# Last pair's attention, output weights and gate: an order of work written differently in a two-layer hybrid attention kernel

## The chip, the cores and the metric

One core of a Trainium2 chip runs the whole program: one launch, no other core takes part. The metric is the device time of an execution in microseconds (us), the median of several executions. Engines are named as in the profile: PE (TensorE's matmuls), PEld (its weight loads), DVE (VectorE), ACT (ScalarE), POOL (GpSimd), SP (SyncE, whose queue issues most of the loads).

## The reference

512 latent tokens and 256 context tokens of width 1024 go through two layers. Each layer modulates a root-mean-square norm with a shift and a scale, projects into three groups of attention heads and a gate path, and adds the gated output projection:

```python
mod = c_silu @ ada_w + ada_b
shift, scale, gate = jnp.split(mod, 3, axis=-1)
hx = rmsnorm(x, norm_w) * (1 + scale[:, None, :]) + shift[:, None, :]
px = split_cols(hx @ w_in)
...
ux = jnp.concatenate([ya, yb, yc_], axis=-1) * jax.nn.silu(px[9])
x = x + gate[:, None, :] * (ux @ w_out)
```

Group A is global attention (8 heads on 2 key heads, normalised and rotated), B is attention to a 2-D neighbourhood with a learned bias, C is a sliding window with a sink logit. All are softmax in float32. The context stream has its own modulation and is dropped after the first layer. The result is the final norm of the latent stream.

## The kernel before, in words

Everything is held transposed, features on the partitions and tokens along the free axis, and float32 products are made of three products of halves: each operand is split into a rounded high half and the rest (weights: `split`, line 239, `wh` by ACT at line 242 and `wl` by DVE or POOL at line 245).

**Stages of a layer.** A first stretch of projections; then the attention of twelve pairs of heads, each beside the projections for later pairs; then the output projection in eight blocks of 128 features. `PLAN` (line 33) lists for each step the pair whose attention runs, the projections beside it, and a couple of counts, for layer 0 and layer 1, of small pieces of modulation work. Its first entry has no pair (`None`), the second is pair (B, 0). `weave` (line 1371) interleaves the two generators in program order: it advances the attention while its cost so far, as a share of its planned cost `ta`, is not ahead of the other's share of `tb`. `with_ada` (line 1449) strews the counted pieces evenly over the projections' planned time.

**The order on the engines.** Instructions are written in program order, and a scheduler then orders each engine's queue by that order and by a model of when operands and buffers are ready. An extra edge, `after` (line 99), forces one instruction behind another of the same queue without a wait. In `weave`, `pace["at"]` is the name of an attention matmul that lies `CFG["lead"]` = 6.0 us of attention cost back; projections place every third of their products behind it (`paced`, line 291). The output products (`out_mm`, line 510) do not read it: only an explicit `behind_mm` counts.

**The last pair and the first output blocks.** The pair (C, 3) has no projections left beside it. The last line of `mixers` (1534) weaves its attention (with what is left of pair (A, 3)) with `head` (line 522): reloads of nine finished head-group results, and the products of output blocks 0 and 1 with eleven of the twelve feature groups, three products (cost 3 x 512/2400 = 0.64 us in the plan) for each group, 66 in all. The planned cost of the attention is 12.5 + 2.7 us in layer 0 and 12.5 us in layer 1, that of `head` 2 x 7.0 and 2 x 3.5. The twelfth group, which needs (C, 3) itself, is added when the block is finished.

**The output blocks of layer 0.** The loop over `d` in `body` (line 729) loads block `d`'s three weight tiles (`load_wo`, line 502: three loads of 256 KB on SP's queue into three staging buffers `ws`, then halves into five buffers `wh` and five `wl`, for blocks 5 to 7 into kept buffers), makes the latent tokens' block and for blocks 2 and 3 at once the context's (`block`, line 554). Blocks 0 and 1 come from `head`. From block 2 on it also works out layer 1's shift on DVE: `dot_begin` (line 692) loads two rows (`row`) and two pieces of modulation weights (`dw`, 512 KB each), `dot_step` makes two dot products (line 153) and loads the piece after next. These loads, and those of the class `Dots` (line 156), go through `aside` (line 141), which puts them behind the latest weight load written (`pace["sp"]`). Pieces, rows and kept weight halves share nine buffers. One step is made per block at block 2 and 3 for each stream, two at each block from the fifth on, until all eight are made.

**Layer 1's gate** is made by `Dots` in steps: sixteen dot products of half a row on DVE and two steps that only wait for the second half's row. Its rows and pieces take two of the four buffers `vt`, which the V tiles of the attention share. `PLAN` gives the first projections of layer 1 twelve steps and the stage of pair (B, 0) six.

Of the kernel before, what the change touches and what calls it, by code (L numbers as in the profile page):

```python
# [20 lines left out]
KT = 8  # L21
# [8 lines left out]
RPAD = 32  # L30
FT_ORDER = (4, 5, 6, 7, 0, 8, 1, 9, 2, 10, 3, 11)

PLAN = [(None, [("g", 0), ("b", 0), ("v", 0)], (0, 12)),
# [12 lines left out]
LATER = (5, 6, 7)  # L46
# [3 lines left out]
CFG = dict(lead=6.0, hp=600, hpf=600, pj=2, T=2, O=1, P=5, qt=5, kt=4, vt=4, gt=3, wh=5, ws=3, pt=3, bm=2, tA=1, OT=1, u=1, tl=1, ab="pj", tR=1, map={}, ada=2, h0=300, h1=1000, a0=9, H=2, hr=0, cp="A", cv="A", w0="D", w1="D", w2=(("D", "D"), ("D", "D")), hb="D", ws_="P")  # L50
# [13 lines left out]
def body(tc, xT, small, bcast, rpb, adaw, adat, wt, wf, wo, trigA, trigC, mskB, mskC, outT):  # L64
# [34 lines left out]
    def after(inst, name):  # L99

        tc.add_manual_dep(inst.ins, name, mybir.DependencyInfo(mybir.DependencyClass.NoSync,
                                                               mybir.DependencyReason.DATA), reason="bank")
# [133 lines left out]
    pace = {"at": None, "pe": None, "dve": None, "sp": None}  # L236
# [142 lines left out]
    with tc.tile_pool(name="p0", bufs=1, reuse_waits="tile") as p0:  # L379
        xs = {}  # L380
# [121 lines left out]
    def load_wo(l, d, room=None):  # L502
        w = {}
        for i in (1, 0, 2):
            st = wpool.tile([128, 512], F32, name="ws", bufs=CFG["ws"])
            pace["sp"] = nc.sync.dma_start(st, wo[l, d, i]).ins.name
            w[i] = split(st, (4, 128), room and room())
        return w

    def out_mm(p, w, ft, c0, n, behind_mm=None):  # L510
        wh, wl = w[ft // 4]
        r = ft % 4
        for i, (a, b) in enumerate(((wh, 0), (wh, 1), (wl, 0))):
            mm = nc.tensor.matmul(p[:, 0:n], a[:, r, :], ucols(ua[b][ft], c0, n),  # L514
                                  start=(ft == FT_ORDER[0] and i == 0), stop=(ft == FT_ORDER[-1] and i == 2))
            if i == 0 and behind_mm:
                after(mm, behind_mm)

    heads = {}
    out_banks = [pj, pj, lambda: Sbig[:, 0:512], psT, psT]  # L520
# [16 lines left out]
    for l in range(2):  # L537
        last = l == 1
        with tc.tile_pool(name=f"p1_{l}", bufs=1, reuse_waits="tile") as p1:
            mixers(tc, nc, l, last, p1, ps, const, dict(locals()))  # L540
        with tc.tile_pool(name=f"p2_{l}", bufs=1, reuse_waits="tile") as p2:
# [12 lines left out]
            def block(d, s, xs, sums, w):  # L554

                c0, c1 = SETS[s]
                n = c1 - c0
                xr = p2.tile([128, NT], F32, name="xr", bufs=3)
                nc.sync.dma_start(xr[:, 0:n], xsrc[l][d][:, c0:c1])
                if s == 0 and d in heads:  # L560
                    p, w = heads.pop(d)
                    fts = FT_ORDER[-1:]
                else:
                    p = out_bank()
                    fts = FT_ORDER
                for ft in fts:
                    out_mm(p, w, ft, c0, n)
                x = p2.tile([128, n], F32, name=f"xn{s}", bufs=8)
                res = nc.vector.scalar_tensor_tensor(x, p[:, 0:n], gate[:, d, s:s + 1], xr[:, 0:n],
                                                     op0=OP.mult, op1=OP.add)  # L570
                add_sq(sums, x, len(xs), n, p2)
                if s == 0:
                    xd = dram.tile([128, NT], F32, name=f"x1_{d}")
                    nc.scalar.dma_start(xd, x)
                    xsrc.setdefault(1, []).append(xd)
                xs[d] = x
                return res
# [108 lines left out]
            xs, sums = ({}, {}), ([], [])  # L686
# [25 lines left out]
            def dot_next():  # L712
                dot_step(dn["n"])
                dn["n"] += 1
# [11 lines left out]


            held = {}
            for d in range(KT):
                w = None  # L730
                if d not in heads:
                    w = load_wo(l, d, kept if d in LATER else None)
                if d == 2:
                    dot_begin()
                block(d, 0, xs[0], sums[0], w)
                for _ in range(0 if d < 2 else 2 if d > 3 else 1):
                    dot_next()
                if w is None or d in LATER or d not in AT_ONCE:
                    held[d] = w if d in LATER else None
                else:  # L740
                    block(d, 1, xs[1], sums[1], w)
                    dot_next()
            factors(0)
            n = 0
            for i, (d, w) in enumerate(sorted(held.items())):
# [11 lines left out]
def mixers(tc, nc, l, last, p1, ps, const, env):  # L757
    g_ = env
    en, pace = g_["en"], g_["pace"]
# [443 lines left out]
    class NearUnit(Unit):  # L1203
# [3 lines left out]

        PLAN = {1: (64, 0, 0, 256, {1: 0, 2: 128, 4: 256, 5: 384}),
# [3 lines left out]

        def scores(self):
            self.P = {}
            for i in (1, 2, 0, 3):
                k0, p0, loc, cx, _ = self.PLAN[i]
                nl = min(256, NT - k0, 128 * i + 192)
# [23 lines left out]
        def values(self):  # L1241
            O = psO()
            for n, kb in enumerate((4, 5, 1, 2, 3, 0)):
                qs = [i for i in range(4) if kb in self.PLAN[i][4]]
                T = psT()
# [89 lines left out]
    def chain(gens):  # L1335
        for g in gens:
            yield from g
# [30 lines left out]
                except StopIteration:  # L1368
                    lb = False

    def weave(a, ta, b, tb):

        xa = xb = 0.0
        la = a is not None
        past = []
        pace["pe"] = None
        while True:
            if la and xa * tb <= xb * ta:
                try:
                    xa += next(a)  # L1380
                    past.append((xa, pace["pe"]))
                except StopIteration:
                    la = False
            else:
                while len(past) > 1 and past[1][0] <= xa - CFG["lead"]:
                    past.pop(0)
                pace["at"] = past[0][1] if past and past[0][0] <= xa - CFG["lead"] else None
                try:
                    xb += next(b)
                except StopIteration as r:  # L1390
                    pace["at"] = None
                    if la:
                        for _ in a:
                            pass
                    return r.value
# [71 lines left out]
    TA = {"A": 16.5, "B": 12.5, "C": 12.5, None: 1.0}  # L1467
    TC = 0.0 if last else 2.7
# [7 lines left out]
    def any_bank():  # L1476
# [9 lines left out]
                g=b_g)  # L1486
# [7 lines left out]
    bmb = bias_b()  # L1494
    for pair, items, n_ada in PLAN:
        if pair is None and not last:

            items = items[1:] + items[:1]
        if pair is not None:
            kind, i = pair  # L1500
# [20 lines left out]
    def rest():  # L1521
        yield from attend(prev)
        yield from chain(pend)

    def urgent(gen):
        while True:
            with tc.high_priority(offset=CFG["hr"]):
                try:
                    x = next(gen)
                except StopIteration:  # L1530
                    return
            yield x

    weave(urgent(rest()), TA["C"] + TC, g_["head"](l, p1), CFG["H"] * (3.5 if last else 7.0))


def col_index():
# [95 lines left out]
```

## Time and profile before

| | us |
|---|---|
| median of 3 runs | 1215.67 |
| lowest, highest | 1214.95, 1218.88 |
| profiled execution, its own time | 1216.13 |
| its span, first to last instruction | 1214.3 |
| mean granted TensorE clock | 0.993 |

The profile is of one execution. Times within it count from the first instruction. A window row gives the length of a stretch, then each engine's busy time with the number of its instructions, the granted TensorE clock (1.00 is 2.4 GHz, 0.50 is 1.2 GHz), the busy share of the 16 DMA engines and what they moved in GB/s. A timeline row gives start and length, the engine and the source line, the operation with its output and inputs by the program's names, how many were merged, and in brackets the engine's idle time just before, with what ended it. Matmuls are pipelined: the start of one and the start of the next tell the pace, not the listed length.

### The profile page before, as it was taken

The page shows a single profiled execution, that of the slowest core. Times are in us where ns is not written, and L with a number is a line of the kernel's source. Part 1 is how long each engine was busy: PE and PEld are TensorE (multiplying, and loading weights), DVE is VectorE, ACT ScalarE, POOL GpSimd, SP SyncE. Part 2 cuts the span into 40 slices and gives each one's busy share as a digit, 9 for nine tenths or more (in the row PEclk, how much of TensorE's full clock was granted, in tenths as well). Part 3 has the DMA queues.
Part 4 walks back from the last instruction along what each step waited for, and adds up shares of the span by engine and source line. Part 5 has one row for each costly group of instructions (what it writes and reads, how often), then busy time and mean ns, then how long its engine had stood idle before and what let it go on. Part 6 is the DMA issues. An engine that isn't in the chain of part 4 may idle for free.

```text
span 1214.3 us, 21741 instructions
## 1 busy us (share of the span) xinstructions
PE 1160.1 (96%) x8016; PEld 1037.9 (85%) x8016; DVE 760.8 (63%) x1541; ACT 697.0 (57%) x1581; POOL 416.3 (34%) x511
## 2 busy tenths in 40 slices
PE   5999999999999999999889999999999999989997
PEld 3898999998898989988768999889989888878776
DVE  5667666765466665567577875666754665556553
ACT  5546555665566576587423544555666666667552
POOL 2432111233455454485100030211364554546001
PEclk9999999999999999999989999999999999999998
DMA  9552222312232112114085662333222112133052
GB/s 329 197 149 82 83 68 93 131 40 90 79 110 83 66 44 96 36 53 126 18 319 179 193 193 79 94 108 97 85 70 62 55 43 69 37 86 89 27 162 73
DMA packets 60826, 124.22 MB, mean 102 GB/s; under 512 B 7216, under 2 KB 13488, under 8 KB 60720
## 3 DMA queue, kind: packets, MB, share of 16 engines
q1 hardware_dynamic: 54768, 111.96, 29.0%
q10 hardware_dynamic: 5952, 10.88, 2.7%
q8 instruction: 63, 1.03, 0.4%
q14 instruction: 43, 0.35, 0.1%
HBM read 109.05 MB, written 11.14 MB: 99 GB/s over the span
## 4 chain that ended last, share of the span: by engine, by line
PE 82%; DVE 6%; ACT 4%; issue 3%; DMA 2%; POOL 1%; SPq 0%; ACTq 0%; DVEq 0%; POOLq 0%
PE pj L313 19%; PE pj L336 17%; PE Sbig L1034 9%; PE Obig L1034 9%; PE T L1039 8%; PE pj L514 5%; PE Sbig L514 3%; PE T L514 3%; PE T L336 2%; PE Sbig L425 1%; DVE ptl L1029 1%; ACT pth L783 1%; PE Sbig L336 1%; PE pj L425 1%; PE pj L209 1%
## 5 line engine op out<-in xcount | busy, mean ns | idle before, releaser
L1029 DVE TENSOR_TENSOR ptl<-T,pth 128x512 fp32r<-128x512 f32 (+2 forms) x312 | 180.8, 590 | 130.4 <-ACT pth L783 128.3
L783 ACT ACTIVATE pth<-T 128x512 fp32r<-128x512 f32 (+2 forms) x312 | 158.8, 519 | 138.7 <-PE T L1039 124.8
L336 PE MATMUL pj<-wh,hL 128*128 128x256 f32 x896 | 179.8, 287 | 0.1
L313 PE MATMUL pj<-hL,wh 128*128 128x512 f32 x544 | 175.9, 401 | 1.3 <-ACT wh L242 0.9
L1039 PE MATMUL T<-ident,P 128*128 128x128 f32 x1024 | 164.8, 273 | 4.8 <-DVE ptl L1029 2.6
L242 ACT ACTIVATE wh<-ws 128x512 fp32r<-128x512 f32 x192 | 119.3, 628 | 75.8 <-PE pj L313 14.4
L1034 PE MATMUL Sbig<-kt,qt 128*128 128x256 f32 (+1 forms) x864 | 157.6, 309 | 2.7 <-DVE negm L1177 1.8
L245 POOL TENSOR_TENSOR wl<-ws,wh 128x512 fp32r<-128x512 f32 x76 | 99.0, 1307 | 152.4 <-ACT wh L242 131.7
L336 PEld LDWEIGHTS pj<-wh,hL 128*128 128x128 f32 x896 | 144.3, 190 | 2.6 <-issue 0.6
L1034 PE MATMUL Obig<-pth,vt 128*128 128x256 f32 (+2 forms) x432 | 133.5, 319 | 8.0 <-ACT pth L783 7.1
L1039 PEld LDWEIGHTS T<-ident,P 128*128 128x128 f32 x1024 | 122.7, 140 | 17.3 <-DVE ptl L1029 3.9
L1034 PE MATMUL Obig<-ptl,vt 128*128 128x256 f32 (+2 forms) x432 | 131.8, 319 | 5.1 <-DVE ptl L1029 4.7
L1034 PEld LDWEIGHTS Sbig<-kt,qt 128*128 128x128 f32 x864 | 123.7, 189 | 13.3 <-DVE negm L1177 3.6
L336 PE MATMUL pj<-wl,hL 128*128 128x256 f32 x448 | 128.4, 287 | 0.0
L313 PEld LDWEIGHTS pj<-hL,wh 128*128 128x128 f32 x544 | 96.4, 189 | 17.6 <-ACT wh L242 1.3
L245 DVE TENSOR_TENSOR wl<-ws,wh 128x512 fp32r<-128x512 f32 x116 | 81.4, 709 | 46.5 <-ACT wh L242 41.0
L313 PE MATMUL pj<-hL,wl 128*128 128x512 f32 x272 | 107.2, 394 | 0.6 <-DVE wl L245 0.6
L1034 PEld LDWEIGHTS Obig<-pth,vt 128*128 128x128 f32 x432 | 81.6, 189 | 19.4 <-ACT pth L783 12.7
L1034 PEld LDWEIGHTS Obig<-ptl,vt 128*128 128x128 f32 x432 | 81.5, 189 | 16.3 <-DVE ptl L1029 11.3
L1409 POOL TENSOR_TENSOR bm<-wr,bm 128x192 f32<-128x192 f32 (+1 forms) x48 | 40.1, 864 | 142.9 <-DMA bm<-mskB_dram 130.2
L336 PEld LDWEIGHTS pj<-wl,hL 128*128 128x128 f32 x448 | 85.3, 190 | 0.4
L1129 DVE TENSOR_REDUCE negm<-Sbig 128x1 f32<-128x768 f32 x64 | 61.1, 955 | 33.9 <-ACT P L1131 20.3
(334 smaller groups left out, 2503.3 us busy)
## 6 DMA issues: line engine op xcount, KB each, us to landing
ws<-wf_dram SPq DMA_DIRECT2D x72, 256.0 KB, 2.9
ws<-wt_dram SPq DMA_DIRECT2D x72, 256.0 KB, 3.0
ada<-adaw_dram SPq DMA_DIRECT2D x32, 512.0 KB, 6.2
ws<-wo_dram SPq DMA_DIRECT2D x57, 256.0 KB, 2.7
bm<-mskB_dram SPq DMA_DIRECT2D x16, 576.0 KB, 3.8
dw<-adat_dram SPq DMA_DIRECT2D x8, 512.0 KB, 9.4
dots<-adat_dram SPq DMA_DIRECT2D x16, 256.0 KB, 3.7
u<-u ACTq DMA_DIRECT2D x9, 384.0 KB, 3.0
```

The source lines that it names most:

```text
L242: nc.scalar.activation(hi, src, AF.Copy)
L245: eng.tensor_sub(lo, src, hi.bitcast(F32))
L313: paced(nc.tensor.matmul(p[:, 0:n], a[:, r, :], cols(b[kt], c0, n), start=(i == 0), stop=(i == 23)), i)
L336: paced(nc.tensor.matmul(p[:, t * 256:(t + 1) * 256], tok(a[kt], t2 + t), b[:, r, :], start=(i == 0), stop=(i == 23)), i)
L425: mm = nc.tensor.matmul(out, a, b, start=begin, stop=(kt == KT - 1 and i == 2), skip_group_check=True)
L514: mm = nc.tensor.matmul(p[:, 0:n], a[:, r, :], ucols(ua[b][ft], c0, n), start=(ft == FT_ORDER[0] and i == 0), stop=(ft == FT_ORDER[-1] and ...
L783: nc.scalar.activation(out, src, AF.Copy)
L1029: i = nc.vector.tensor_sub(lo[:, 0:n], T[:, 0:n], hi[:, 0:n].bitcast(F32))
L1034: m = nc.tensor.matmul(*args, **kw)
L1039: m = nc.tensor.transpose(*args, **kw)
L1129: nc.vector.tensor_reduce(nm, S, axis=AX.X, op=OP.max, negate=True)
L1409: nc.gpsimd.tensor_add(b, src, b)
```

## The change

In layer 1 all eighteen steps of the gate go into the first projections, none beside (B, 0). The products of `head` read `pace["at"]`, and the last weave is given a lead of 3.0 us instead of 6.0 and the planned cost of `head` 2 x 8.0 us in layer 0 and 2 x 7.5 us in layer 1. In layer 0's output loop the weight load of block `d` + 1 is written at the start of step `d`, and the eight steps of dots follow a table: one behind each stream's block 2, one and two behind block 3, three behind block 4.

```diff
-PLAN = [(None, [("g", 0), ("b", 0), ("v", 0)], (0, 12)),
-        (("B", 0), [("b", 1)], (0, 6)),
+PLAN = [(None, [("g", 0), ("b", 0), ("v", 0)], (0, 18)),
+        (("B", 0), [("b", 1)], (0, 0)),
...
-            if i == 0 and behind_mm:
-                after(mm, behind_mm)
+            if i == 0 and (behind_mm or pace["at"]):
+                after(mm, behind_mm or pace["at"])
...
+            ws_ = {}
+
+            def load_next(d):
+
+                if d < KT and d not in heads:
+                    ws_[d] = load_wo(l, d, kept if d in LATER else None)
+
+            n_dots = {(2, 0): 1, (2, 1): 1, (3, 0): 1, (3, 1): 2, (4, 0): 3}
+
+            def out_block(d, s, w):
+                block(d, s, xs[s], sums[s], w)
+                for _ in range(n_dots.get((d, s), 0)):
+                    dot_next()
+
             for d in range(KT):
-                w = None
-                if d not in heads:
-                    w = load_wo(l, d, kept if d in LATER else None)
+                load_next(d + 1)
                 if d == 2:
                     dot_begin()
-                block(d, 0, xs[0], sums[0], w)
-                for _ in range(0 if d < 2 else 2 if d > 3 else 1):
-                    dot_next()
+                w = ws_.get(d)
+                out_block(d, 0, w)
                 if w is None or d in LATER or d not in AT_ONCE:
                     held[d] = w if d in LATER else None
                 else:
-                    block(d, 1, xs[1], sums[1], w)
-                    dot_next()
+                    out_block(d, 1, w)
...
-    def weave(a, ta, b, tb):
+    def weave(a, ta, b, tb, lead=CFG["lead"]):
...
-                while len(past) > 1 and past[1][0] <= xa - CFG["lead"]:
+                while len(past) > 1 and past[1][0] <= xa - lead:
                     past.pop(0)
-                pace["at"] = past[0][1] if past and past[0][0] <= xa - CFG["lead"] else None
+                pace["at"] = past[0][1] if past and past[0][0] <= xa - lead else None
...
-    weave(urgent(rest()), TA["C"] + TC, g_["head"](l, p1), CFG["H"] * (3.5 if last else 7.0))
+    weave(urgent(rest()), TA["C"] + TC, g_["head"](l, p1), CFG["H"] * (7.5 if last else 8.0), 3.0)
```

## Rows read from the trace of the kernel before

**Rows 1.** The page, part 1: busy time, share of the span, instructions

```profile
PE 1160.1 (96%) x8016; PEld 1037.9 (85%) x8016; DVE 760.8 (63%) x1541; ACT 697.0 (57%) x1581; POOL 416.3 (34%) x511
```

**Rows 2.** Windows, last pairs: length, busy PE PEld DVE ACT POOL, PEclk, DMA

```profile
565.00:605.00 40.00, 36.05 (x196) 29.36 (x196) 22.70 (x49) 20.75 (x51) 5.90 (x8) 0.96 0.09 29
...
1122.00:1160.00 38.00, 35.28 (x202) 29.03 (x201) 22.42 (x48) 19.77 (x44) 1.48 (x4) 1.00 0.08 28
...
590.00:595.00 5.00, 5.00 (x15) 3.92 (x16) 1.20 (x4) 0.76 (x2) 2.21 (x6) 0.66 0.00 0
```

**Rows 3.** The same view: stretches of earlier pairs, for comparison

```profile
500.00:540.00 40.00, 38.74 (x263) 34.60 (x262) 24.69 (x46) 31.24 (x75) 26.40 (x32) 1.00 0.17 48
...
1085.00:1095.00 10.00, 8.00 (x45) 6.20 (x45) 5.14 (x9) 7.93 (x19) 5.64 (x8) 1.00 0.31 81
```

**Rows 4.** Windows, output products of line 514 alone, before the last pair's scores

```profile
549.00:562.50 13.50, 8.28 (x32) 5.73 (x32) 1.00 0.68 187
...
1096.00:1121.50 25.50, 11.31 (x39) 6.95 (x39) 1.00 0.36 102
```

**Rows 5.** Timeline of PE, layer 0's output blocks

```profile
630.44 0.73 PE L514 MATMUL pj<-hL,wh 128*128 128x512 f32 x2 [3.09 <-ACT wh L242]
...
633.15 0.79 PE L514 MATMUL pj<-hL,wl 128*128 128x512 f32 x1 [1.97 <-DVE wl L245]
...
637.43 0.83 PE L514 MATMUL pj<-kt,wh 128*128 128x512 f32 x2
...
641.09 3.56 PE L514 MATMUL Sbig<-hL,kept 128*128 128x512 f32 x15
```

**Rows 6.** Timeline of SP's queue, same stretch

```profile
581.73 27.03 SPq L506 DMA_DIRECT2D ws<-wo_dram  x3
...
609.80 0.86 SPq L143 DMA_DIRECT2D row<-spread  x2
...
610.71 0.90 SPq L143 DMA_DIRECT2D dw<-adat_dram  x2
...
613.38 2.22 SPq L143 DMA_DIRECT2D dw<-adat_dram  x3
...
619.73 0.33 SPq L143 DMA_DIRECT2D dw<-adat_dram  x1
...
623.27 1.93 SPq L506 DMA_DIRECT2D ws<-wo_dram  x2
```

**Rows 7.** Windows, all engines, same stretch

```profile
620.00:630.00 10.00, 7.36 (x42) 6.13 (x40) 9.89 (x17) 1.29 (x3) 0.00 (x0) 1.00 1.03 382
...
630.00:640.00 10.00, 7.59 (x22) 5.36 (x23) 10.00 (x18) 4.15 (x8) 0.00 (x0) 0.66 0.88 312
```

**Rows 8.** DVE's group of line 153 (layer 1's shift), 607 to 655 us

```profile
L153 DVE CUSTOM_DVE_ANT_0 junk<-dw,row,sm 128x1024 bf16<-128x1024 f32 x16 | 20.4, 1277 | 0.1
```

**Rows 9.** Windows, all engines, layer 1's first projections and first pair

```profile
683.00:700.00 17.00, 15.53 (x108) 14.09 (x106) 16.49 (x37) 7.52 (x20) 0.79 (x1) 1.00 0.54 177
...
728.00:746.00 18.00, 18.00 (x127) 16.60 (x126) 7.44 (x14) 6.45 (x13) 0.00 (x0) 1.00 0.28 83
...
770.00:775.00 5.00, 3.87 (x24) 2.60 (x21) 5.00 (x16) 3.77 (x11) 0.15 (x1) 1.00 0.31 106
...
775.00:780.00 5.00, 4.68 (x30) 3.89 (x31) 4.81 (x14) 3.63 (x12) 3.76 (x8) 1.00 0.04 15
```

**Rows 10.** Windows, line 153 alone (two records each)

```profile
762.00:775.00 13.00, 3.91 (x10) 1.00 0.27 73
```

**Rows 11.** Timeline of PE and ACT, layer 1's first pair

```profile
778.72 0.36 PE L336 MATMUL pj<-wh,hC 128*128 128x256 f32 x1
...
774.62 0.67 ACT L783 ACTIVATE vt<-pj 128x256 fp32r<-128x256 f32 x2
```

**Rows 12.** Timeline of PE, layer 1's last pair

```profile
1136.81 0.50 PE L1034 MATMUL Obig<-pth,vt 128*128 128x512 f32 x1 [1.26 <-ACT pth L783]
...
1138.79 0.73 PE L514 MATMUL pj<-qt,wh 128*128 128x512 f32 x2
```


## The prediction

> **What bounds the kernel.** I read the page's busy times first: TensorE (PE) is busy 1160.1 us, 96% of the span, and the next engine 63% [rows 1]. So an edit pays only where it removes idle time of PE or time in which PE runs at its lower clock. Going through the span in windows, I looked for such time inside the stages that the diff touches, and found three kinds.
>
> First, the attention of the last pair (C, 3). In layer 0, PE is idle 3.95 us of the 40 us from 565 [rows 2], and in five of these microseconds the granted clock is 0.66 [rows 2], a mixture of 2.4 and 1.2 GHz, right behind idle pieces; that costs 0.34 x 5 = 1.7 us. In layer 1 the same attention has 2.72 us idle of 38, at full clock [rows 2]. For comparison, an earlier stretch in which paced projections lie evenly beside attention loses 1.26 of 40 us, 3.15%, and a poorly filled one 2.00 of 10, 20% [rows 3].
>
> Second, layer 0's output blocks. The timeline shows PE waiting 3.09 us for a weight tile's high half and 1.97 us for its low half [rows 5]. Behind the wait nine products, from 633.15 to 637.43, take 4.28 us [rows 5]; fifteen later ones take 3.56, of which the last is 0.39, so one follows another by 3.17/14 = 0.226 us [rows 5], and the nine lose 4.28 - 9 x 0.226 = 2.25 us to the lower clock (0.66 in that window [rows 7]). Together 7.3 us. The queue of SP says why: the two loads were issued at 623.27, behind two rows and six pieces of modulation weights (two from 610.71, three from 613.38, one at 619.73) [rows 6].
>
> Third, layer 1's first pair: PE is idle 1.13 + 0.32 = 1.45 us from 770 to 780, with VectorE (DVE) full [rows 9]; the projection's products come back only at 778.72, after the copies into V at 774.62 [rows 11]. Five dots lie in these 13 us (ten records) [rows 10], and the dots hold two of the four buffers that V needs.
>
> **The change, part by part.**
>
> (1) Products behind the last pair, layer 0. No product is added or removed; 66 of them (two blocks x 11 x 3) get a place in PE's order. Before, 32 were done ahead of the pair's scores [rows 4]. Of the new order the first 3.0 us of attention cost set no anchor: 3.0 x 16/15.2 = 3.2 us of product cost, at 0.64 per three products five groups, 15 products. So 17 products, 17 x 0.226 = 3.8 us, move from before the pair into its attention. Gross gain: the 3.95 + 1.7 lost there [rows 2], less the 3.15% that such a mixture keeps (1.26) [rows 3]: 4.4 us. Cost: the earlier stretch loses 3.8 us of filler. It lies between nothing (the rest closes up) and 3.8 us (all of it idle); I take the 20% of the poorly filled row [rows 3], 0.8, because that is also an attention with one projection beside it. Net -3.6.
>
> (2) The same in layer 1. 39 products came before the scores [rows 4]; 3.0 x 15/12.5 = 3.6 us, or 18 products, may stay; 21 x 0.226 = 4.7 us move. Gross 2.72 - 1.2 = 1.5, cost 20% of 4.7 = 0.9 (bounds 0 and 4.7). Net -0.6.
>
> For both, the rows show PE standing 1.26 us for a value product at 1136.81, with products of the head coming at 1138.79 [rows 12]: a wait at the front of PE's order is paid whatever stands behind it. The Trainium skill, PSUM — Partial Sum Buffer, Engine vs sequencer instructions, says that matmuls start and complete in program order; by it a product anchored behind an attention matmul also stands behind each of that matmul's waits. The trace agrees in that piece. By this rule alone (1) and (2) could gain nothing, and the sum would be -6.5 instead of -10.7; it is a rival below. I don't take it, because an anchor is an instruction 3 us of cost earlier, normally done by then.
>
> (3) Output weights ahead of modulation loads. The load of block d + 1 is written ahead of the dots and the row loads of block d, and modulation loads are anchored to the latest weight load written. Hence the fifth block's weights stand behind two rows and four pieces instead of six; the two others, 0.52 MB each, are 2.7 us at 382 GB/s [rows 7], and SP no longer waits for their turn. Nothing is added: eight steps of dots stay eight, but all lie ahead of the sixth block's products, not the last of them behind. Beside them SP also issues the residual rows; these loads come at most three weight loads later and are wanted only at a block's end. What is late next is DVE: it is busy 19.89 of the 20 us around the stall [rows 7], has 20.4 us of dots to do beside the weights' low halves [rows 8], and works in order. One wait of 1.97 us for a low half [rows 5] I leave in place. Bounds: 0 and 7.3. Net -(7.3 - 2.0) = -5.3.
>
> (4) Layer 1's gate in the first projections. Eighteen steps instead of twelve there, none beside the first pair. The five dots and what was still to load for them move to about 728 to 746. They are 3.91 us of DVE [rows 10], where DVE has 10.6 us free of 18 and PE is full [rows 9], so I cost them at nothing; if they fell into 683 to 700, where DVE is busy 16.49 of 17 us and PE already idles 1.47 [rows 9], they might double that. Freed: 1.45 us, less some rest: net -1.2 (bounds -1.45 and +1.5).
>
> Sum: -3.6 - 0.6 - 5.3 - 1.2 = -10.7 us. The profiled execution took 1216.13 us (span 1214.3), so 1205.4; the median of the runs lies 0.46 below it, so **1205.0 us**. A measurement of this kernel can tell about 0.3% from no change, 3.6 us: faster is under 1212.0, slower over 1219.3.
>
> **Rivals.**
>
> A, VectorE takes over the output blocks (0.20): the wait for a low half comes in three blocks, 3 x 1.97 = 5.9 instead of 2.0. For: DVE is full there, and three dots more lie ahead of the later blocks' halves. Against: its row loads, issued behind a 27 us entry of SP's queue [rows 6], can now start earlier. -6.8, 1208.9 us.
>
> B, PE's order keeps the waits (0.15): products stand behind the attention's own waits, a wait at the front is paid whatever stands behind it, and (1) and (2) give nothing net. The rule named above would have it so. For: the piece at 1136.81 [rows 12]. Against: the slack of 3 us. -6.5, 1209.2.
>
> C, the change doesn't do what (3) says (0.15): the fifth block's weights find no free staging or split buffer until the blocks before are done, and come as late as now. For: SP's entry that stood from 581.73 to 608.76 was one of its three weight loads waiting for such a buffer [rows 6]. Against: once it was through, the loads behind it were the modulation's. -5.4, 1210.3.
>
> D, slower (0.06): the stretches ahead of the last pairs starve. All 3.8 + 4.7 us that leave them become idle, and the clock falls once in each, at 1.7 us [rows 2]: +11.9, with (1) and (2) gaining nothing. Against (3) and (4), -6.5, this is +5.4: 1221.1. It decides once these losses exceed 6.5 + 3.6 = 10.1. For: 20% idle beside one projection [rows 3]; against: no stretch here loses more.
>
> E, only (4) works (0.07): -1.2, 1214.5.
>
> **How the numbers follow.** The forecast has 0.37. Faster than 1212.0 are the forecast, A, B and most of C, 0.85; unknown sizes take off some: 0.81. Same 0.12, slower 0.07. Below, all that is lost in these places is 5.65 + 2.72 + 7.3 + 1.45 = 17.1 us, so 1198.5; I end the range at 1199. Above, it takes in A, B and C and ends at 1212, which leaves out E and D. The forecast's own range is 1201 to 1208.
>
> **What would show it.** (1): PE idle under 2 us in the last pair's attention of layer 0, no clock below 1.00 there, and the third block's products behind the attention instead of inside it. (2): about 1 us more idle ahead of layer 1's last pair and 1.5 less in it. (3): the fifth block's weight loads issued ahead of the last four pieces, and no wait over 2 us there. (4): all sixteen dots before 746, no gap at 770 to 780. I am wrong if block 5 or 6 waits for DVE instead, or if PE idles longer where the products were taken away.

## The result, and the profile after

The changed kernel takes 1207.66 us (median of 4 runs, 1206.50 to 1208.72) beside 1215.59 before; the two medians lie 7.9 us apart. The ratio on record is 0.9923, with an interval of 0.9899 to 0.9946, which is 9.4 us less (6.6 to 12.3). Twelve further runs stand below; each has its own kernel before on the same chip, so each is given as a ratio to that. Executions of one and the same kernel differ by some 4 us (17 of the kernel before on one chip: 1214.0 to 1218.4), and the profiled ones differ by up to 3.9 us in the first 530 us already, where no edit reaches (runs 3 and 6 have a granted clock of 0.83 from 20 to 30 us, others have 1.00). Therefore I compare traces by stages and not by spans. Two executions of the kernel before that took 1286 and 1885 us are left out, and the profiled one of run 12 took 2881 us, so that run has no row in the table below.

The page's first part, after, answers to [rows 1]: TensorE (PE) has the same work in a shorter span.

```profile
PE 1159.1 (96%) x8016; PEld 1037.9 (86%) x8016; DVE 766.0 (64%) x1541; ACT 697.7 (58%) x1581; POOL 418.3 (35%) x511
```

The stages are bounded by six instructions that every kernel has, here in the timelines of DVE and PE of the changed kernel: the finish of the pair before the last two of layer 0, of its last pair, the first sum of squares behind the output blocks, and the finishes of layer 1's fourth, ninth and last pair.

```profile
531.04 0.68 DVE L1326 SCALAR_TENSOR_TENSOR OT<-OT,T 128x512 f32<-128x512 f32 x1
...
601.74 0.69 DVE L1326 SCALAR_TENSOR_TENSOR OT<-OT,T 128x512 f32<-128x512 f32 x1
...
663.48 0.73 PE L354 MATMUL Obig<-ones,sq 128*128 128x2 f32 x6
...
908.73 0.68 DVE L1332 SCALAR_TENSOR_TENSOR u<-OT,T 128x512 f32<-128x512 f32 x1
...
1063.29 0.69 DVE L1332 SCALAR_TENSOR_TENSOR u<-OT,T 128x512 f32<-128x512 f32 x1
...
1150.76 0.69 DVE L1326 SCALAR_TENSOR_TENSOR OT<-OT,T 128x512 f32<-128x512 f32 x1
```

The same instructions, taken from each kernel's trace, give this table (us; each stage is the difference of two such starts; the parts of the prediction fall into the stages P, O, F and L):

| kernel | to 531 | P: last two pairs, layer 0 | O: output blocks | F: layer 1 to the fourth pair | pairs 5 to 9 | L: last three pairs |
|---|---|---|---|---|---|---|
| before | 529.7 | 74.96 | 65.34 | 247.42 | 154.8 | 87.96 |
| changed | 531.0 | 70.70 | 61.74 | 245.25 | 154.6 | 87.47 |
| 1 gate alone | 530.0 | 73.47 | 63.87 | 245.01 | 154.7 | 88.87 |
| 2 loads alone | 529.7 | 74.96 | 61.67 | 246.92 | 154.6 | 87.91 |
| 3 order alone | 533.2 | 70.49 | 65.04 | 246.26 | 154.6 | 87.16 |
| 4 costs without ties | 530.0 | 73.60 | 65.54 | 246.35 | 154.7 | 88.96 |
| 5 ties without costs | 531.1 | 70.88 | 64.78 | 246.28 | 155.3 | 89.90 |
| 6 dots' old places | 533.6 | 70.62 | 62.87 | 244.64 | 154.6 | 87.29 |
| 7 half dots | 533.2 | 70.72 | 61.04 | 248.16 | 155.9 | 86.94 |
| 8 low halves on GpSimd | 533.5 | 70.84 | 66.06 | 245.34 | 154.5 | 87.21 |
| 9 stores from GpSimd | 531.2 | 70.68 | 62.16 | 244.54 | 154.6 | 86.07 |
| 10 half loads | 533.0 | 70.75 | 57.36 | 245.48 | 154.5 | 88.31 |
| 11 early pieces | 529.8 | 70.62 | 62.77 | 244.68 | 154.6 | 87.29 |

Changed against before: -4.26, -3.60, -2.17, -0.21 and -0.49, together -10.7 us, of which the slower start of that execution takes back 1.3: the span fell by 9.4.

Each row is one execution, and a stage that a run leaves alone shows how far such a row can be trusted. O, with the loads as before, lies between 63.87 and 65.54 (before and runs 1, 3, 4, 5); L, with the order as before, between 87.91 and 88.87 (before and runs 1, 2). A difference of 1 to 1.5 us in one row is not yet an effect.

**P and L, the last pairs.** All-engine windows of the changed kernel, moved by the 3 and 9.4 us that it is ahead (length, busy PE, PEld, DVE, ACT, POOL, clock, transfers):

```profile
562.00:602.00 40.00, 38.87 (x230) 33.18 (x229) 25.36 (x53) 23.43 (x55) 9.81 (x15) 1.00 0.15 46
1112.60:1150.60 38.00, 36.93 (x212) 30.97 (x210) 21.35 (x46) 19.75 (x43) 1.49 (x5) 1.00 0.13 35
```

PE idles 1.13 us in layer 0's last pair, where it idled 3.95 at a clock of 0.96, and 1.07 in layer 1's, where it was 2.72 [rows 2].

L has one thing that the kernel before does not have. From 1080 to 1090, two pairs ahead of the end, the granted clock of the changed kernel is 0.78 and then 0.88, where before it is 1.00. Run 9, whose edit does not touch this stage, has 1.00 there, and its L is 86.07, 1.4 us shorter. The windows of PE alone, first the changed kernel and then run 9:

```profile
1080.00:1085.00 5.00, 4.00 (x16) 0.78 0.60 162
```

```profile
1080.00:1085.00 5.00, 4.03 (x20) 1.00 0.59 162
```

**O, the output blocks.** The timeline of PE:

```profile
624.79 0.73 PE L514 MATMUL pj<-hL,wh 128*128 128x512 f32 x2 [0.38 <-ACT wh L242]
...
627.98 0.50 PE L514 MATMUL pj<-hL,wl 128*128 128x512 f32 x1 [1.50 <-DVE wl L245]
...
628.79 0.57 PE L514 MATMUL pj<-hL,wl 128*128 128x512 f32 x1
...
632.43 0.39 PE L514 MATMUL pj<-ut,wl 128*128 128x512 f32 x1
```

The waits of 3.09 and 1.97 us [rows 5] are now 0.38 and 1.50. But nine products, from 628.79 to 632.43, still take 3.64 us instead of 9 x 0.226 = 2.03: 1.6 us of the lower clock are still there, as the windows of PE alone show (busy, clock, transfers' share, GB/s):

```profile
625.00:630.00 5.00, 3.50 (x11) 0.88 1.03 395
630.00:635.00 5.00, 5.00 (x19) 0.77 0.59 210
```

SP's queue, changed:

```profile
606.86 0.85 SPq L143 DMA_DIRECT2D row<-spread  x2
607.76 0.90 SPq L143 DMA_DIRECT2D dw<-adat_dram  x2
...
610.22 1.21 SPq L143 DMA_DIRECT2D dw<-adat_dram  x2
611.66 0.37 SPq L506 DMA_DIRECT2D ws<-wo_dram  x1
...
618.26 0.33 SPq L506 DMA_DIRECT2D ws<-wo_dram  x1
...
619.83 2.92 SPq L143 DMA_DIRECT2D dw<-adat_dram  x3
```

The weights that PE waited for are the fifth block's second and third tile. (Its first tile was loaded at 605.48, and before at 608.43; where a text below speaks of the fifth block's first weights, the second tile is meant.) They are asked for at 611.66 and 618.26, behind two rows and four pieces and ahead of the last four; before it was 623.27 and 624.87, behind six [rows 6].

**F, layer 1's first projections.** The gap of [rows 9] is gone (windows of all engines; the kernel is some 6 to 9 us ahead here, and from 755 to 790 PE idles 0.10 us in all). The last dot starts at 722.6, not at 773.6:

```profile
770.00:775.00 5.00, 4.97 (x33) 4.34 (x33) 5.00 (x10) 4.50 (x11) 2.84 (x6) 1.00 0.81 272
775.00:780.00 5.00, 4.93 (x27) 4.03 (x27) 3.57 (x9) 2.48 (x6) 1.90 (x3) 1.00 0.51 108
```

### The profile page after: what moved, and what is told of

Its sections match the earlier page's. It is cut to its first block, busy times and chain, and to the rows that moved or that the text cites. A ratio compares the mean times of both kernels' runs of the same rounds, so it can differ in the third digit from the quotient of the medians.

```text
span 1204.9 us, 21753 instructions
## 1 busy us (share of the span) xinstructions
PE 1159.1 (96%) x8016; PEld 1037.9 (86%) x8016; DVE 766.0 (64%) x1541; ACT 697.7 (58%) x1581; POOL 418.3 (35%) x511
## 3 DMA queue, kind: packets, MB, share of 16 engines
q8 instruction: 63, 1.03, 0.3%
## 4 chain that ended last, share of the span: by engine, by line
PE 83%; DVE 6%; ACT 4%; DMA 3%; issue 3%; POOL 0%; ACTq 0%; SPq 0%; DVEq 0%; POOLq 0%
PE pj L313 19%; PE pj L336 17%; PE Sbig L1044 10%; PE Obig L1044 9%; PE T L1049 9%; PE pj L514 4%; PE T L514 3%; PE Sbig L514 3%; PE T L336 2%; PE Sbig L425 1%; DVE ptl L1039 1%; ACT pth L793 1%; PE pj L425 1%; PE Sbig L336 1%; PE pj L209 1%
## 5 line engine op out<-in xcount | busy, mean ns | idle before, releaser
L245 DVE TENSOR_TENSOR wl<-ws,wh 128x512 fp32r<-128x512 f32 x116 | 85.2, 741 | 43.3 <-ACT wh L242 39.4
```

Of the source, the lines that this page charges most:

```text
L245: eng.tensor_sub(lo, src, hi.bitcast(F32))
```

## Experiments: each part alone

The theory is that the three parts add up and that each works by the mechanism in the prediction. The rivals: the order's gain comes from weights that arrive earlier, or the parts need each other.

**1. The gate alone.** Before, with

```
-PLAN = [(None, [("g", 0), ("b", 0), ("v", 0)], (0, 12)),
-        (("B", 0), [("b", 1)], (0, 6)),
+PLAN = [(None, [("g", 0), ("b", 0), ("v", 0)], (0, 18)),
+        (("B", 0), [("b", 1)], (0, 0)),
```

> The kernel before with part (4) alone: the gate's 18 projection steps stand in layer 1's first projections, none of them in the first pair. By the sum of the prediction this is worth 1.2 us: 1214.4 beside 1215.6. In the changed kernel the stretch from the first normalized columns of layer 1 to the third pair's result fell by 2.2 to 2.4 us; if all of that is the gate's, this run is at 1213.3. If the change's parts depend on one another (the dots end 50 us earlier only where the output blocks take them), it stays within 0.5 us of the kernel before. In the trace: the five microseconds 770 to 775 and 775 to 780, where TensorE was busy 3.7 and 4.4 us, filled to 4.9; the first pair's result some 5 us later, the second's and third's earlier.

Measured: 1215.62 beside 1217.06, ratio 0.9988 (0.9977 to 0.9999): 1.5 us less, between 0.1 and 2.8. The gap is filled:

```profile
770.00:775.00 5.00, 4.97 (x43) 1.00 0.28 67
775.00:780.00 5.00, 5.00 (x29) 1.00 0.72 242
```

(The stretch that the expectation ends at the third pair ends at the fourth, stage F.) F fell by 2.41, but runs 2 to 5, which leave the gate where it was, also have 0.5 to 1.2 less than the one profiled execution of before. Taking means, the six kernels with the gate's edit and whole dots have 244.91 in F, the five without it 246.65: 1.7 us are the gate's.

This run shows something else: P is 1.5 us shorter, with nothing changed there. Before, the window 590 to 595 had a clock of 0.66 [rows 2]; here it is 1.00 (PE alone):

```profile
590.00:595.00 5.00, 4.76 (x23) 1.00 0.00 0
```

O is 1.5 us shorter too, again with nothing changed: PE waits 2.3 us for the high half, where it waited 3.09 [rows 5].

**2. The loads alone.** Before, with

```
+            def load_next(d):
+                if d < KT and d not in heads:
+                    ws_[d] = load_wo(l, d, kept if d in LATER else None)
+            n_dots = {(2, 0): 1, (2, 1): 1, (3, 0): 1, (3, 1): 2, (4, 0): 3}
...
-                    w = load_wo(l, d, kept if d in LATER else None)
+                load_next(d + 1)
```

> The kernel before with part (3) alone: the next block's output weights are asked for ahead of the modulation pieces, and the sixteen dots stand behind other blocks. The sum of the prediction gives 5.3 us (1210.3); the changed kernel's output blocks were 3.6 us shorter than before (1212.0 if the part is independent of the order in the last attention). Rival: the weights find no free staging buffer before the pieces are consumed, and nothing is gained (1215.6). In the trace: the wait of 3.09 us for the high half of the fifth block's first weights falls below 0.5; a wait of 1.5 to 2 us for its low half, on VectorE, stays; one stretch of 3.4 us at half clock in place of 6.8.

Measured: 1212.07, ratio 0.9961 (0.9946 to 0.9976): 4.7 us less (2.9 to 6.6). O is 61.67, as in the changed kernel (61.74), so the part doesn't need the others. PE's waits from 606 to 662 (us in total, times, longest) and its clock:

```profile
PE pj L514 <- DVE wl L245: 1.5, 1, 1.5
PE pj L514 <- ACT wh L242: 0.3, 1, 0.3
```

```profile
630.00:635.00 5.00, 4.19 (x11) 0.66 0.96 361
```

Both are as expected: the high half is waited for 0.3 us only, the low half 1.5, and one stretch of the lower clock stays.

**3. The order alone.** Before, with

```
-            if i == 0 and behind_mm:
-                after(mm, behind_mm)
+            if i == 0 and (behind_mm or pace["at"]):
+                after(mm, behind_mm or pace["at"])
...
-    weave(urgent(rest()), TA["C"] + TC, g_["head"](l, p1), CFG["H"] * (3.5 if last else 7.0))
+    weave(urgent(rest()), TA["C"] + TC, g_["head"](l, p1), CFG["H"] * (7.5 if last else 8.0), 3.0)
```

> The kernel before with parts (1) and (2) alone: output blocks' products tied to the attention's steps, with lead 3.0 and the costs 8.0 and 7.5 in both layers. The sum of the prediction gives 3.6 + 0.6 = 4.2 us (1211.4); the changed kernel's trace showed 4.3 + 0.5 = 4.8 (1210.8). Rival: the gain came from weights that arrive earlier, not from the order; then it is under 1 us. In the trace: no clock below 1.00 between 560 and 605 and TensorE busy above 4.9 us in each five microseconds from 565 to 600.

Measured: 1211.30, ratio 0.9955 (0.9940 to 0.9969): 5.5 us less (3.8 to 7.3). The rival falls, since the weights arrive as before. P and L are 4.47 and 0.80 shorter. PE alone, in the same 40 us of the last pair:

```profile
564.00:604.00 40.00, 38.87 (x232) 1.00 0.16 47
```

1.5 + 4.7 + 5.5 = 11.7 us beside 9.4 (6.6 to 12.3) for all together: the parts add up within their intervals.

**4. Its costs without the ties.** As run 3, without the edit of the products' helper.

> As the run before, but without the anchors: the products of the output blocks are costed at 8.0 and 7.5 and woven with lead 3.0, and TensorE's order against the attention is left to the scheduler. If the tie of each first product to the attention's step does the work, nothing is gained here (1215.6, or above it: the two output blocks are then spread thinner but still go wherever they are ready); if the costs alone do it, 4 to 5 us are gained (1211). I lean to the tie: about 1 us gained, 1214.5, and the five microseconds 590 to 595 still show a clock below 1.00.

Measured: 1216.19, ratio 0.9992 (0.9978 to 1.0007). The tie is needed, as I leaned. The products are not spread:

```profile
585.00:590.00 5.00, 3.13 (x21) 1.00 0.14 48
590.00:595.00 5.00, 4.76 (x24) 1.00 0.00 0
```

PE idles 1.87 us in the first window, as before, and yet the clock stays at 1.00 in the second: my mark for the clock was wrong. P is 73.60 here, 73.47 in run 1, and 74.96 in run 2 and before, all four without the ties. So 1.4 us of P is a stretch of the lower clock that two of these traces have and two have not, and the order's own part is 73.5 - 70.7 = 2.8. (With one trace of each kernel, it is not shown whether the kernel or the execution decides.)

**5. The ties without the costs.** As run 3, with the old 3.5 and 7.0 in the call of the weave.

> The kernel before with the ties of the output blocks' products and lead 3.0, but with the old costs 7.0 and 3.5. With the costs alone the last attention of layer 0 lost only the half clock (TensorE still idle for 1.9 us in 585 to 590). If the ties do the work by themselves, this run is at the time of the order's whole edit (0.9955 of before, 1210 to 1212); if the costs decide where the tied products fall, it gives part of it in layer 0 (7.0 against 8.0 is near) and none in layer 1 (3.5 against 7.5): 0.5 to 1 us more than the whole edit.

Measured: 1216.02, ratio 0.9995 (0.9984 to 1.0006). I was wrong by about 4 us. In layer 0 the ties alone do all (P is 70.88, 2.7 less than in runs 1 and 4). Layer 1 gives most of that back: L is 89.90, 1.9 more than before and 2.4 more than the changed kernel; some 0.7 less is left, and the times have 0.6 less (from 1.9 less to 0.7 more). The output products (line 514 alone) that fell ahead of layer 1's last pair show why. The windows are moved so that each ends as far ahead of the last pair's finish as 1121.5 does before. First this run, then the changed kernel:

```profile
1094.10:1119.60 25.50, 2.49 (x8) 1.00 0.27 74
```

```profile
1086.60:1112.10 25.50, 5.82 (x18) 1.00 0.34 94
```

The longest waits of PE in this run, from 1096 to 1150:

```profile
PE Obig L1034 <- DVE OT L1057: 1.5, 1, 1.5
PE Sbig L1034 <- DVE negm L1177: 1.2, 1, 1.2
```

Before, 11.31 us of products lay there [rows 4]. At a cost of 3.5 a block the weave asks for the products so late, against the attention's steps, that the stretch ahead of the last pair is left nearly bare, and PE idles 3.75 us of it; the cost of 7.5 leaves 18 products (5.82 us) there, and PE idles 1.70, beside 1.05 before. That is my rival D, in one layer.

## Experiments: what limits the output blocks now

O fell by 3.6 us where I forecast 5.3. My prediction names VectorE as what is late next. Rivals: ScalarE's queue, the places of the dots, the transfers.

**6. The dots where they were.** The changed kernel, with

```
-            n_dots = {(2, 0): 1, (2, 1): 1, (3, 0): 1, (3, 1): 2, (4, 0): 3}
+            n_dots = {(2, 0): 1, (2, 1): 1, (3, 0): 1, (3, 1): 1, (4, 0): 2, (5, 0): 2}
```

> The changed kernel with the weights asked for ahead, but the dots where they were before (one behind each of blocks 2 and 3, two behind blocks 4 and 5). It splits part (3) into its two edits. If the earlier request does the work, the time stays at the changed kernel's 1207.7; if the dots' new places are needed (they set when the pieces' buffers come free), 2 to 4 us come back: 1210 to 1212. I lean to the first, with the low halves of the fifth block's weights 1 us earlier (fewer dots stand ahead of them on VectorE), so 1206.5 to 1207.7.

Measured: 1207.24, ratio 0.9930 (0.9906 to 0.9953), the changed kernel's time. The earlier request does the work; O is 1.1 longer in this one trace, which is within what such rows vary by, and the times don't show it.

**7. Half the dots' work.** The changed kernel, with half of each sum left out:

```
-                        dot(1, 0, j, s, 0, dw[j], rows[s], p2)
+                        dot(1, 0, j, s, 0, dw[j][:, 0:512], rows[s][:, 0:512], p2)
```

> The changed kernel in which each of the sixteen dots of layer 1's shift sums only the first 512 of its 1,024 products: half of that sum is left out, the pieces are still loaded whole. Each dot falls from 1.28 to about 0.75 us, VectorE's work in the output blocks by 16 x 0.53 = 8.5 us. If VectorE is what is now late in the output blocks (the wait of 1.50 us for the low half of the fifth block's weights, and the stretch of 3.4 us at half clock behind it), that wait goes and with it the 1.7 us of the half clock: 3 us less, 1204.5. If ScalarE's splits or the transfers are late, under 0.5 us changes: 1207.5.

Measured: 1208.48, ratio 0.9948 (0.9929 to 0.9967), not 1204.5. With 8.5 us less on VectorE, O is only 0.7 shorter, and PE still waits 2.2 us, though no five microseconds from 605 to 650 have a clock below 1.00:

```profile
PE pj L514 <- DVE wl L245: 1.0, 1, 1.0
PE Sbig L514 <- DVE kept L245: 0.6, 1, 0.6
PE pj L514 <- ACT wh L242: 0.6, 1, 0.6
```

Three halves are late in turn, on two engines: what they share must come earlier. VectorE's work is not the limit. (Stage F is 2.9 us longer than the changed kernel's; why is left open.)

**8. Low halves on GpSimd.** The changed kernel, with `w2=(("DP", "D"), ...)` in place of `w2=(("D", "D"), ...)`.

> The changed kernel with every other low half of layer 0's output weights made on GpSimd in place of VectorE. If VectorE's queue of dots is what the low halves of the fifth block wait for, GpSimd (idle there) makes at least one of two in time: 1 to 3 us less, 1205 to 1206.7. If a low half takes longer on GpSimd than it waits on VectorE (as it shares VectorE's data with it), the wait only moves: 1207.7 to 1210.

Measured: 1212.36, ratio 0.9969 (0.9955 to 0.9983): some 5 us more than the changed kernel. The group of line 245 (duration in ns, least, median, most):

```profile
L245 POOL TENSOR_TENSOR wl<-ws,wh x6: 1284/1292/1303, 609.9 to 660.5; 128x512 fp32r<-128x512 f32 x6
...
L245 DVE TENSOR_TENSOR kept<-ws,kept x5: 675/680/1735, 634.8 to 652.9; 128x512 fp32r<-128x512 f32 x5
L245 POOL TENSOR_TENSOR kept<-ws,kept x4: 1617/2024/2281, 636.0 to 650.8; 128x512 fp32r<-128x512 f32 x4
```

A low half takes 1.3 to 2.3 us on GpSimd and 0.68 on VectorE (median), and one of VectorE's took 1.74.

**9. Stores from GpSimd's queue.** The changed kernel, with

```
-                    nc.scalar.dma_start(xd, x)
+                    nc.gpsimd.dma_start(xd, x)
```

> The changed kernel with the stores of layer 1's input columns (one behind each output block) issued from GpSimd's queue in place of ScalarE's. ScalarE sat idle for 3.5 us ahead of the split of the fifth block's first weights, with such a store standing ahead of it in its queue. If the store's wait holds the split back, the split comes 2 to 3 us earlier, and the wait of the products falls to what VectorE's low half leaves (1.50 us): up to 0.4 us less at TensorE, and up to 2 if the half clock stretch goes with it (1205.7 to 1207.3). If the split only waits for its load, nothing changes: 1207.7.

Measured: 1206.34, ratio 0.9925 (0.9906 to 0.9945): no gain that can be told. ScalarE is free earlier, and now waits for the weights themselves:

```profile
622.56 0.63 ACT L242 ACTIVATE wh<-ws 128x512 fp32r<-128x512 f32 x1 [1.53 <-DMA ws<-wo_dram]
...
625.03 0.63 ACT L242 ACTIVATE wh<-ws 128x512 fp32r<-128x512 f32 x1 [0.75 <-DMA ws<-wo_dram]
```

The split of the fifth block's second tile begins at 622.56 instead of 624.11, that of the third at 625.03 instead of 624.95: the store was one delay, the transfer stands right behind it.

PE waits here for a low half as long as in the changed kernel, and behind the wait there is no lower clock:

```profile
628.10 0.50 PE L514 MATMUL pj<-hL,wl 128*128 128x512 f32 x1 [1.50 <-DVE wl L245]
...
628.90 0.40 PE L514 MATMUL pj<-hL,wl 128*128 128x512 f32 x1
...
630.95 0.39 PE L514 MATMUL pj<-ut,wl 128*128 128x512 f32 x1
```

The nine products from 628.90 take 2.05 us, where the same nine took 3.64. O is no shorter for it (62.16), since PE's waits for low halves add up to 3.1 us here.

**10. Half the loads too.** Run 7, and in addition

```
-                    aside(dw[j], adat[DOT_AT[1, 0] + j])
+                    aside(dw[j][:, 0:512], adat[DOT_AT[1, 0] + j, :, 0:512])
```

> The run with half of each dot, and in addition only that half of each modulation piece is loaded: 2 MB less in the output blocks of layer 0 (half of the shift's sum is left out, as there). There the transfers moved about 400 GB/s from 612 to 632 us with the 16 engines busy throughout, so 2 MB are some 5 us of them. If the transfers are what the output blocks wait for now, the remaining waits for split weights go, no clock below 1.00 is left between 605 and 645, and the stretch from layer 0's last head results to layer 1's first transpose falls from 61.0 us (halved dots, whole loads) by 2 to 4. If ScalarE's or VectorE's queue is, it stays within 0.5 us.

Measured: 1202.99, ratio 0.9891 (0.9875 to 0.9906). Against run 7 only the bytes differ, and O falls by 3.68 us, from 61.04 to 57.36, inside the 2 to 4 expected. PE waits for nothing from 606 to 662, and its windows are full at full clock:

```profile
620.00:625.00 5.00, 5.00 (x33) 1.00 1.05 387
625.00:630.00 5.00, 5.00 (x24) 1.00 1.00 360
630.00:635.00 5.00, 5.00 (x24) 1.00 0.72 209
635.00:640.00 5.00, 5.00 (x24) 1.00 0.83 277
```

No other kernel's O is below 61.04. So what is left of the output blocks' loss are the transfers: from 615 to 630 in the changed kernel the 16 engines are full, at 376 to 408 GB/s, and weights, pieces, rows and residuals share them. Both runs have half of VectorE's dots; with whole dots and half the bytes VectorE might come next, which no run tried. (F is back at 245.48, which is as little explained as its length in run 7.)

**11. The pieces earlier.** The changed kernel, with

```
-                if d == 2:
+                if d == 0:
                     dot_begin()
+                load_next(d + 1)
...
-            n_dots = {(2, 0): 1, (2, 1): 1, (3, 0): 1, (3, 1): 2, (4, 0): 3}
+            n_dots = {(1, 0): 1, (2, 0): 1, (2, 1): 1, (3, 0): 1, (3, 1): 2, (4, 0): 2}
```

(the request of the next weights stands behind `dot_begin` instead of ahead).

> The changed kernel with the modulation rows and the first two pieces asked for ahead of the first output block, where the transfers were idle from 585 to 605 us, and the first dot behind the second block's latents. If the transfers are the limit of the output blocks and the pieces' buffers are free by then, some 2 MB move out of the crowded 20 us: 1 to 3 us less, 1205 to 1206.7, and the wait of 1.50 us goes. If the buffers are still the attention's, the queue that issues the weights stands behind the pieces, and the third block's weights come late: 2 to 10 us more, 1210 to 1218.

Measured: 1206.10, ratio 0.9918 (0.9904 to 0.9931), beside 0.9922 for the changed kernel on the same chip (run 12): no difference. The pieces did not get into the idle time, as SP's queue shows:

```profile
577.51 26.96 SPq L506 DMA_DIRECT2D ws<-wo_dram  x4
604.52 0.90 SPq L143 DMA_DIRECT2D row<-spread  x2
605.52 0.85 SPq L143 DMA_DIRECT2D dw<-adat_dram  x2
```

Four weight loads of the earlier blocks hold the queue for 27 us, each waiting for a low half to be split off and so for its staging buffer, as before [rows 6], and the pieces stand behind them. They come only 2.2 us earlier, 1.3 of which is this execution's earlier start; the crowd moves with them, and PE still waits 2.7 us for split weights and a finished block. So this run does not try what it was meant to try; a queue of their own for the pieces is what it leaves open. No run here beat the changed kernel with the whole computation.

**12. The changed kernel again.**

> The changed kernel itself, beside the run with the early pieces on one chip: 0.9923 of the kernel before within the interval of 0.9899 to 0.9946. If the early pieces gain, they are 1 to 3 us below this one.

Measured: 1207.94, ratio 0.9922 (0.9907 to 0.9936), the same as at first.

## Why the prediction was right

1205.0 was forecast with 1199 to 1212, and 1207.7 came out: the direction held, and so did the three parts, each of which gains when it is alone. The sizes of (1), (2) and (3) did not, and what (3) says is late next was wrong. That the stages' sum of -10.7 is the same number as the forecast's is luck.

**(1), order in layer 0: -3.6 forecast, -4.3 in the trace.** PE's idle time in the last pair fell from 3.95 to 1.13 us, close to the 1.26 that I left it. But I put the 1.7 us of the lower clock down to the idle pieces ahead of it. Runs 1 and 4 have the same idle pieces at a clock of 1.00. So of -4.3 some 1.4 are a clock that differs between these traces, and 2.8 the order's, where my term without the clock was 3.95 - 1.26 - 0.8 = 1.9. PE's idle time in the whole of P fell from 4.1 to 2.6, so the earlier stretch paid 1.3 and not 0.8; where the other 1.3 of the 2.8 come from, the windows don't show, as they count PE busy there. One mark failed: the third block's products still stand inside the attention's end, from 588.78 to 598.39, not behind it; it did no harm.

**(2), order in layer 1: -0.6 forecast, -0.5 in the trace.** This agreement is luck. Both marks came nearly so: the pair itself lost 1.65 us of idle time, and the stretch ahead gained 0.65 (1.05 to 1.70 of 25.5), where the sum took 0.9; 18 products stayed ahead, as I had worked out. But the changed kernel's L also holds the lower clock from 1080 to 1090, which I had not reckoned with. Run 9, without it, has an L 1.9 us below the kernel before, so the term was too small by about 1.3. Run 5 shows how much hangs on the cost: the same ties with the weave's old one make that end of the kernel 1.9 us longer than before.

**(3), loads: -5.3 forecast, -3.6 in the trace.** This is the term that was mis-sized most. The waits came out as I wrote: 0.38 + 1.50 = 1.88 where I kept 1.97. What I did not keep is the lower clock behind a wait: I let all 2.25 us of it go with the longer wait, and 1.6 stayed in the changed kernel and 1.7 in run 2. In this trace that is enough: 5.3 - 1.6 = 3.7. It is not a fixed price, since run 9 has the same wait of 1.50 us and none of it. The 7.3 us that I started from were one execution's, too: runs 1, 3, 4 and 5, with the loads as before, wait 3.8 to 4.4 us there, not 5.06, and against the mean of the five O with the old loads, 64.91, the changed kernel and run 2 gain 3.2. The times of run 2 have 2.9 to 6.6. "What is late next is DVE" was wrong too. Its windows are full [rows 7] and the last releaser of the wait is DVE, but run 7 took 8.5 us off it and gained 0.7 in this stage, and run 10 then took 2 MB off the transfers and gained 3.7. The row that should have told me stood in the same windows: transfers at 1.03 of their engines and 382 GB/s.

**(4), the gate: -1.2 forecast, -1.5 (0.1 to 2.8) alone,** and 1.7 by the means of stage F. The dots that moved lie between 699 and 723, somewhat ahead of the place that I gave them; PE is full there (14.93 us of the 15 from 693.5, 13.00 of the 13 from 708.5), and they cost nothing, as assumed.

The rivals. A (VectorE takes over) falls with the one wait of 1.50 us, where it asked for three, and with run 7. B (PE's order keeps the waits) falls with run 3: the Trainium skill, PSUM — Partial Sum Buffer, Engine vs sequencer instructions, states that matmuls complete in program order, and the trace doesn't contradict that, yet run 3 gains 5.5 us. That a product tied to a step of the attention does not inherit that step's wait, because the step is done by then, is my reading of it. C falls with SP's entries at 611.66 and 618.26. D happened only in run 5. E falls with runs 2 and 3.

## What to carry to other kernels

Where two streams are woven by estimated costs, a tie and the cost that places it are one edit: here each alone gave nothing (0.9992 and 0.9995), both together 0.9955. When an engine is full and is also the last to release a wait, look at the transfers of that window before blaming it: a full VectorE could lose 8.5 us of work without effect while the 16 transfer engines were full as well. And a stretch of the lower clock in one trace is not a price to be added up: behind the same wait of 1.50 us the changed kernel lost 1.6 us to it and run 9 nothing. Before such a stretch enters a sum, look whether the traces of other kernels, with the same work there, have it too.

## What the runs showed of the hardware

A stretch of the lower clock is no fixed consequence of the idle pieces ahead of it. Without the ties, 1.9 us of idle time in the five from 585 were followed by a clock of 1.00 in runs 1 and 4, and by 0.66 and 0.67 in the kernel before and in run 2. From 1080 to 1085, PE was busy 4.00 us at 0.78 in the changed kernel and 4.03 us at 1.00 in run 9; and behind a wait of 1.50 us nine products took 3.64 us in the one and 2.05 in the other. Even the first 530 us, with the same work in all kernels, differ by up to 3.9 us between the traces. The clock explains this in part at most: runs 3 and 6 have 0.83 from 20 to 30 us, but runs 7, 8 and 10 are as late with 1.00.

In run 8, GpSimd's cost of one and the same subtraction on 128x512 was 1.29 us in the six cases with the result in the split buffers and 2.02 (1.62 to 2.28) in the four with the kept ones, beside medians of 0.69 and 0.68 on VectorE. VectorE's operations were held up beside some of them: two of its sixteen dots took 1.97 and 2.19 us, the others 1.27 to 1.29. Why is not settled by these runs.
